# Longer yields for the mixer streams, and MoBA's rotary tied behind the end of RWKV's triangular inverse

## The chip, the cores and the metric

The kernel runs on one core of a Trainium2 chip. The metric is the device time of one execution in microseconds (us); the median of three runs of the kernel before is 927.18 us. PE is the matmul engine (TensorE), DVE the vector engine, ACT the scalar engine, POOL is GpSimd, and SP issues most of the DMAs. Every engine runs its own list of instructions in the order in which the built program holds them, and waits at an instruction until what it reads is there.

## The reference

A trunk of two layers on 256 tokens of width 1024, in float32. In each layer a normed input h is projected once, and the columns go to four token mixers of width 256 and to four gates of width 1024:

```python
y_n = mixer_n(h @ W_in)            # n: stick-breaking attention, RWKV-7, MoBA, HGRN2
mix = sum(sigmoid(gate_n(h)) * (y_n @ W_br[n]) for n in range(4))
x   = x + mix @ W_out
x   = x + swiglu_ffn(rms_norm(x))
```

MoBA attention has four heads of 64. Of each head's query and key the first 16 columns are rotated before the scores:

```python
x1, x2 = t[..., :half], t[..., half:ROPE_DIM]
t = concatenate([x1 * cos - x2 * sin, x2 * cos + x1 * sin, t[..., ROPE_DIM:]])
```

RWKV-7 is a recurrence with a matrix state, S_t = S_{t-1} diag(w_t) + (S_{t-1} a_t) b_t^T + v_t k_t^T and y_t = S_t r_t. The kernel computes it in two chunks of 128 tokens, c = 0 and 1, which needs the inverse of a triangular matrix per chunk and head. HGRN2 is a gated linear recurrence, followed by an RMS norm per head and an output gate.

## The kernel before

**Weights and matmuls.** A float32 weight of 128x1024 is loaded by SP (`load_raw`), rounded to fp32r by a cast on ACT (L128, `hi`), and what the rounding lost is subtracted out on DVE (L129, `lo`). Each product is three matmuls: hi by h-high, lo by h-high, hi by h-low. In the listings a projection therefore shows as `pa<-hi,h` and `pa<-lo,h` at L80 (the one line that issues matmuls; L89 issues transposes). Four raw buffers and four split pairs are in use at a time, and three accumulators `pa`.

**A layer.** `phase` holds the projections, gates and branches as a list of units, and two streams that run beside them: one is RWKV, the other is stick-breaking attention, then MoBA, then HGRN. `merge` and `ffn` follow when units and streams are empty. The mixer stretch is about 50 to 251 us in layer 0 and 503 to 705 us in layer 1.

**What sets the order.** `drive` writes the program. It keeps a model clock pe[0], advanced by an estimate for each matmul. A stream yields a number, its estimate of how long the other engines will need, and is taken up again when pe[0] has passed that number times LATK, 1.7. Until then `drive` issues the next step of a unit. So larger yields put more projection matmuls between two steps of a stream. The clock exists only while the program is being built. On the engines other than PE the instructions then stand in an order that the building framework makes from priorities and dependences; `tc.issue_after(x)` ties what is issued within it behind instruction x.

**RWKV around the change.** `pair_scores` (L530 to 542) makes four matmuls and two predicated copies on DVE (L542); it is called for LB (c = 0, 1), and, after LB has been sent through DRAM to `xb`, for LK (c = 0, 1). The inverse of the small triangular blocks (L571 to 598) is a chain of DVE multiplies (L592) and reduces (L595) over 64 partitions, in three levels. Its result `yb` goes to DRAM (L600) and comes back as `cb` (L603), both issued on ACT's queue, and L607 spreads it over blocks, L617 transposes. The last steps, per chunk, end at L788, with a yield of 200 at L790; `y_T` (L792) transposes the output and splits it into `y` high and low.

**MoBA and HGRN.** MoBA's rotary is L981 to L984 for query and key: a shuffle on DVE, a multiply with sin on DVE, one with cos on POOL, an add on DVE. Then, for the token halves t = 0 and 1, scores (L924 to 930), softmax (L991 to 998), a yield, transposes (`flip_att`), the product with v. HGRN's projection ends in `use_n` (L811 to 814: two reads of the accumulator on ACT, a multiply on DVE, one on POOL); L813 frees its accumulator. Its stream runs seven levels and ends, for t = 0 and 1, in products (L903, L905), a square on ACT (L907), a reduce (L909), an inverse root (L262 on DVE, L263 on POOL), two multiplies (L912, L913), a yield of 3500 (L916) and `y_T` (L917). A branch unit (L1019 to 1034) multiplies a mixer's `y` with its weight, as soon as that `y` is there by the model.

Of the kernel before, what the change touches and what calls it, by code (L numbers as in the profile page):

```python
# [15 lines left out]
OP = mybir.AluOpType  # L16
AX = mybir.AxisListType
# [22 lines left out]
SWAP = [*range(8, 16), *range(8), *range(16, 32)]  # L40
# [6 lines left out]
def trunk(ctx, tc, x, w_t, w_n, w_br, w_out, w_gu, w_dn, par, lora, rows, gains, consts, masks, out):  # L47
    nc = tc.nc
# [14 lines left out]
    def g2d(t, a):  # L63
        return t.rearrange("p (a t) -> p a t", a=a)
# [4 lines left out]
    def over(t, n):  # L69
        return t[:, None, :].to_broadcast([128, n, t.shape[-1]])  # L70
# [124 lines left out]
    for i in range(20):  # L195
        nc.tensor.matmul(warm[:, 0:256], flat1[:, 0:128], flat1[:, 0:256], start=True, stop=True)
        if i in (8, 12):
            c = (i - 8) // 4
# [10 lines left out]
    cosT = cn[:, K_COS:K_COS + 256]  # L209
    sinT = cn[:, K_SIN:K_SIN + 256]  # L210
# [52 lines left out]
        nc.gpsimd.tensor_tensor(dst, dst, half[:, :dst.shape[-1]], op=OP.pow)  # L263
        return e

    last, tail, y1 = [None, None], [], []

    def norm_stats(t):
        y = sb("b2", D)
# [195 lines left out]
    def rwkv(m, l, yT):  # L465
# [100 lines left out]
        for c in range(2):  # L566
            LK.append(g2d(sb("b1", 1024), 4))
            pair_scores(kh, LK[c], c)
            yield 2400
        yield 500  # L570
        nc.vector.tensor_copy(yb.rearrange("p s t -> p (s t)")[:, 1::34],  # L571
                              xb.rearrange("p s t -> p (s t)")[:, 1::34])
        tmp = sb("xy", 512)[0:64]
# [1 line left out]
        for lev in range(1, 4):  # L575
            hb = 1 << lev
            nb = 8 // hb

            def blk(q, i, j):
                return bass.AP(tensor=q.tensor, offset=q.offset + i * hb * 16 + j * hb,  # L580
                               ap=[q.ap[0], [34 * hb, nb], [16, hb], [1, hb]])

            pr = tmp[:, 0:nb * hb ** 3].rearrange("p (b i c k) -> p b i c k", b=nb, i=hb, c=hb)
            t4 = th[:, 0:nb * hb * hb].rearrange("p (b i c) -> p b i c", b=nb, i=hb)
            parts = [(slice(None), i) for i in range(hb)] if hb < nb else [(b, slice(None)) for b in range(nb)]
            bc = [64, nb if hb < nb else hb, hb, hb]

            def product(dst, l4, r4):
                r4 = r4.rearrange("p b k c -> p b c k")
                for b, i in parts:  # L590
                    r = r4 if hb < nb else r4[:, b, None]
                    nc.vector.tensor_tensor(pr[:, b, i], l4[:, b, i, None].to_broadcast(bc), r.to_broadcast(bc),  # L592
                                            op=OP.mult)
                for b, i in parts:
                    nc.vector.tensor_reduce(dst[:, b, i], pr[:, b, i], axis=AX.X, op=OP.add)  # L595

            product(t4, blk(yb, 0, 0), blk(xb, 0, 1))
            product(blk(yb, 0, 1), t4, blk(yb, 1, 1))
# [132 lines left out]
        for c in range(2):  # L731
            p = ps("p1")
            for hp in range(2):
                for a in (2 * hp, 2 * hp + 1):
                    d = slice(a * 64, (a + 1) * 64)
                    mm_cols(p[:, d], LK[c][:, a, 0:128], vn[:, c, d], a == 0, c == 0 and a == 3)
                if c:
                    mm(p[:, hp * 128:(hp + 1) * 128], AR[:, 2 * hp + c, 0], st[:, hp], False, hp == 1)
            rh = sb("h1", 256)
            nc.scalar.copy(rh, p[:, 0:256])  # L740
            yield 1000
            p = ps("p1")
            for a in range(4):
                d = slice(a * 64, (a + 1) * 64)
                mm_cols(p[:, d], Y[c][:, a], rh[:, d])
            u = sb("h1", 256)
            nc.scalar.copy(u, p[:, 0:256])
            yield 1000
            if c == 0:
                p = ps("p1")  # L750
                for a in range(4):
                    o = p[hrow(a), (a // 2) * 64:(a // 2) * 64 + 64]
                    d = slice(a * 64, (a + 1) * 64)
                    mm(o, bkn[:, 0, d], u[:, d], True, False)
                    mm(o, bkn[:, 1, d], vn[:, c, d], False, True)
                st = g2d(sb("h1", 256), 2)
                nc.gpsimd.memset(st, 0.0)
                for hp in range(2):
                    for e in range(2):
                        s = hrow(e)  # L760
                        nc.vector.tensor_scalar(st[s, hp, s], p[s, hp * 64:(hp + 1) * 64], fac[s, hp:hp + 1],
                                                None, op0=OP.mult)
            p = ps("p1")
            for hp in range(2):
                for a in (2 * hp, 2 * hp + 1):
                    d = slice(a * 64, (a + 1) * 64)
                    mm_cols(p[:, d], LK[c][:, a, 128:256], vn[:, c, d], a == 0, False)
                if c:
                    mm(p[:, hp * 128:(hp + 1) * 128], AR[:, 2 * hp + c, 1], st[:, hp], False, False)
                for a in (2 * hp, 2 * hp + 1):  # L770
                    d = slice(a * 64, (a + 1) * 64)
                    mm_cols(p[:, d], LB[c][:, a, 128:256], u[:, d], False, a == 3)
            yv = g2d(p[:, 0:256], 4)
            mean = sm.tile([128, 4], F32, name="mean")
            nc.vector.tensor_reduce(mean, yv, axis=AX.X, op=OP.add)
            nc.vector.tensor_scalar(mean, mean, 1.0 / 64, None, op0=OP.mult)
            yc = sb("h1", 256)
            ycv = g2d(yc, 4)
            nc.vector.tensor_tensor(ycv, yv, bcast(mean, 64), op=OP.subtract)
            y2 = sb("h1", 256)  # L780
            nc.scalar.activation(y2, yc, AF.Square)
            var = sm.tile([128, 4], F32, name="var")
            nc.vector.tensor_reduce(var, g2d(y2, 4), axis=AX.X, op=OP.add)
            rsqrt_small(var, var, 1.0 / 64, 64e-5)
            nc.vector.tensor_tensor(ycv, ycv, bcast(var, 64), op=OP.mult)
            nc.vector.tensor_tensor(yc, yc, gnw, op=OP.mult)
            nc.vector.tensor_tensor(yc, yc, bonus[:, c], op=OP.add)
            nc.vector.tensor_tensor(yc, yc, g[:, c], op=OP.mult)  # L788
            ys.append(yc)
            yield 200  # L790
        yield 6000
        yT[1] = y_T(ys, "p1"), pe[0] + 2500  # L792

# [25 lines left out]
    def hgrn(m, l, yT):  # L819
# [79 lines left out]
        for t in range(2):  # L899
# [13 lines left out]
            nc.vector.tensor_tensor(y, y, gs[:, t], op=OP.mult)  # L913
            ys.append(y)
            yield 300
        yield 3500  # L916
        yT[3] = y_T(ys, "p2"), pe[0] + 2500  # L917

    def scores(q, k, t, mask):
# [56 lines left out]

    def moba(m, v, yT):
        r = []
        for u in m:
            o = g2d(sb("c2", 512), 2)  # L980
            nc.vector.stream_shuffle(o, g2d(u, 2), SWAP)  # L981
            nc.vector.tensor_tensor(o, o, over(sinT, 2), op=OP.mult)
            nc.gpsimd.tensor_tensor(g2d(u, 2), g2d(u, 2), over(cosT, 2), op=OP.mult)
            nc.vector.tensor_tensor(o, o, g2d(u, 2), op=OP.add)  # L984
            r.append(o)
        yield 5000
        po = ps("p3")
        for t in range(2):
# [7 lines left out]
                                     accum_out=den[:, a:a + 1])  # L996
            nc.vector.reciprocal(den, den)
            nc.vector.tensor_tensor(z, z, bcast(den, n), op=OP.mult)
            yield 5000 + 2500 * t
            ts = []  # L1000
            flip_att(z, t, ts)
            yield 1200
# [294 lines left out]
```

## Time and profile before

| | before |
|---|---|
| median of 3 runs | 927.18 us (926.2 to 927.2) |
| the profiled execution | 927.26 us |
| its span, first to last instruction | 925.5 us |
| PE busy | 905.9 us, 98% |
| DVE busy | 647.4 us, 70% |
| ACT busy | 475.2 us, 51% |
| POOL busy | 84.7 us, 9% |
| TensorE's mean granted clock | 0.999 |

The span leaves out some 1.8 us of the execution's own time, before the first and behind the last instruction. PE's row counts an instruction from its start to its modelled end; consecutive matmuls overlap, so that a gap is best read from the starts of neighbours. Idle time of another engine costs nothing unless PE waits for what comes out of it.

### The profile page before, as it was taken

How to read it: one execution, taken by the hardware profiler on the slowest of the kernel's cores; microseconds unless marked ns; L12 is line 12 of the kernel's file. 1: busy time of each engine (PE TensorE's matmuls, PEld its weight loads, DVE VectorE, ACT ScalarE, POOL GpSimd, SP SyncE). 2: the span in 40 equal slices, each digit the busy share in tenths (PEclk: the TensorE clock that was granted, in tenths of full speed). 3: DMA queues.
4: the chain of work that ended last, by engine and by line, in shares of the span. 5: the costliest groups of instructions: out<-in, count | busy, mean ns of one | idle time of the engine just before them, and what ended most of it. 6: DMA issues, size and time to landing. Idle time of an engine off the chain costs nothing.

```text
span 925.5 us, 15008 instructions
## 1 busy us (share of the span) xinstructions
PE 905.9 (98%) x5902; PEld 758.4 (82%) x5902; DVE 647.4 (70%) x957; ACT 475.2 (51%) x726; POOL 84.7 (9%) x94
## 2 busy tenths in 40 slices
PE   8999999999999999999999999999999999999996
PEld 5999677778888888888889986777887888888885
DVE  6668877876766666668567778867778566666665
ACT  6564375355535455556345636644455445545453
POOL 3011100333000000000000201032230000000000
PEclk9999999999999999999999999999999999999999
DMA  8644453345864566667435544433467356656551
GB/s 308 222 147 152 121 169 128 102 155 176 266 205 138 181 190 196 182 204 267 144 115 160 161 138 144 142 123 124 131 211 253 112 184 204 189 184 195 182 182 46
DMA packets 50424, 158.11 MB, mean 171 GB/s; under 512 B 9393, under 2 KB 11953, under 8 KB 50354
## 3 DMA queue, kind: packets, MB, share of 16 engines
q1 hardware_dynamic: 43632, 155.19, 52.7%
q10 hardware_dynamic: 6722, 1.97, 0.9%
q8 instruction: 46, 0.75, 0.3%
q14 instruction: 24, 0.20, 0.1%
HBM read 154.91 MB, written 2.23 MB: 170 GB/s over the span
## 4 chain that ended last, share of the span: by engine, by line
PE 83%; DVE 8%; DMA 4%; issue 2%; ACT 2%; POOL 0%; SPq 0%; ACTq 0%; POOLq 0%; DVEq 0%
PE pa L80 58%; PE p L80 23%; DVE lo L129 2%; DMA raw<-in_w_n_dram 1%; PE p L89 1%; PE pa L89 1%; DMA h<-flat 1%; DMA tri<-yb 1%; DMA flat<-b 1%; DMA raw<-in_w_gu_dram 1%; DVE b L966 1%; ACT hi L128 0%; DVE b L542 0%; DVE c L129 0%; DVE c L981 0%
## 5 line engine op out<-in xcount | busy, mean ns | idle before, releaser
L129 DVE TENSOR_TENSOR lo<-raw,hi 128x1024 fp32r<-128x1024 f32 x268 | 330.2, 1237 | 162.6 <-ACT hi L128 159.7
L128 ACT CAST hi<-raw 128x1024 fp32r<-128x1024 f32 x268 | 279.1, 1048 | 238.5 <-PE pa L80 118.4
L80 PE MATMUL pa<-h,hi 128*128 128x256 f32 (+1 forms) x1280 | 277.9, 339 | 0.0
L80 PEld LDWEIGHTS pa<-h,hi 128*128 128x128 f32 x1280 | 215.9, 190 | 24.6 <-issue 2.0
L80 PE MATMUL pa<-hi,h 128*128 128x512 f32 x576 | 193.4, 400 | 2.2 <-DVE p L813 2.2
L80 PE MATMUL pa<-h,lo 128*128 128x256 f32 x960 | 179.9, 283 | 0.0
L80 PEld LDWEIGHTS pa<-h,lo 128*128 128x128 f32 x960 | 148.6, 191 | 7.0 <-issue 0.7
L80 PEld LDWEIGHTS pa<-hi,h 128*128 128x128 f32 x576 | 108.1, 188 | 27.6 <-DVE p L813 3.0
L80 PE MATMUL p<-hi,c 128*128 128x512 f32 (+1 forms) x352 | 113.4, 394 | 0.0
L80 PE MATMUL pa<-lo,h 128*128 128x512 f32 x288 | 112.7, 391 | 0.0
L80 PEld LDWEIGHTS p<-hi,c 128*128 128x128 f32 x352 | 66.1, 189 | 15.2 <-DVE c L129 0.6
L80 PE MATMUL p<-lo,c 128*128 128x512 f32 (+1 forms) x176 | 69.2, 393 | 0.0
L80 PEld LDWEIGHTS pa<-lo,h 128*128 128x128 f32 x288 | 54.2, 188 | 10.0 <-issue 0.3
L263 POOL TENSOR_TENSOR rs<-rs,half 128x1 f32<-128x1 f32 x10 | 6.0, 595 | 471.6 <-DVE rs L262 471.6
L80 PE MATMUL pa<-hi,y 128*128 128x512 f32 x128 | 43.9, 399 | 0.0
L80 PE MATMUL p<-hi,b 128*128 128x512 f32 x128 | 41.5, 396 | 0.2 <-DVE b L129 0.2
L80 PEld LDWEIGHTS p<-lo,c 128*128 128x128 f32 x176 | 33.1, 188 | 6.8
L1034 POOL TENSOR_TENSOR p<-p,gt 128x512 f32<-128x512 f32 x16 | 31.2, 1973 | 54.3 <-DVE gt L1032 54.3
L340 DVE TENSOR_TENSOR gt<-gt,pa 128x256 f32<-128x256 f32 x80 | 33.1, 414 | 0.0
L128 ACT CAST c<-xy 128x512 fp32r<-128x512 f32 x20 | 12.4, 620 | 39.2 <-DVE xy L1137 39.2
L339 ACT COPY gt<-pa 128x256 f32<-128x256 f32 x80 | 29.3, 366 | 0.0
L80 PEld LDWEIGHTS pa<-hi,y 128*128 128x128 f32 x128 | 24.0, 188 | 6.3 <-issue 1.0
(276 smaller groups left out, 936.5 us busy)
## 6 DMA issues: line engine op xcount, KB each, us to landing
raw<-in_w_gu_dram SPq DMA_DIRECT2D x88, 512.0 KB, 3.7
raw<-in_w_n_dram SPq DMA_DIRECT2D x80, 512.0 KB, 3.5
raw<-in_w_dn_dram SPq DMA_DIRECT2D x44, 512.0 KB, 3.5
raw<-in_w_t_dram SPq DMA_DIRECT2D x40, 512.0 KB, 3.6
raw<-in_w_br_dram SPq DMA_DIRECT2D x16, 512.0 KB, 3.6
raw<-in_w_out_dram SPq DMA_DIRECT2D x16, 512.0 KB, 4.4
b<-in_gains_dram SPq DMA_DIRECT2D x4, 512.0 KB, 5.2
flat<-b ACTq DMA_DIRECT2D x4, 256.0 KB, 3.2
```

The lines of the kernel that those rows point to most:

```text
L80: nc.tensor.matmul(o, l, r, start=start, stop=stop)
L89: nc.tensor.transpose(o, i, ident)
L128: a = nc.scalar.copy(dst[0], src)
L129: return a, (eng or nc.vector).tensor_tensor(dst[1], src, dst[0], op=OP.subtract)
L263: nc.gpsimd.tensor_tensor(dst, dst, half[:, :dst.shape[-1]], op=OP.pow)
L339: nc.scalar.copy(dst, p[:, 256:512])
L340: nc.vector.tensor_tensor(dst, dst, p[:, 0:256], op=OP.add)
L966: nc.vector.tensor_tensor_scan(kb, kb, reset[t][:, ::-1], 1.0, op0=OP.mult, op1=OP.add)
L1034: e.tensor_tensor(mg[f, t], mg[f, t], g, op=OP.add)
```

## The change

The list `inv` carries the last reduce of the inverse from the RWKV stream to the MoBA stream. MoBA waits in steps of 1000 until it is set, ties the rotary of query and key behind it, and clears it. The yields become longer: 3200 instead of 2400 behind each pair of LK scores, with the yield of 500 behind them dropped; 1500 and 200 instead of 200 and 200 at the end of RWKV's two chunks; 6800 and 8300 instead of 5000 and 7500 behind MoBA's softmax; 4300 instead of 3500 ahead of HGRN's `y_T`. No instruction is added to the arithmetic and none is dropped. From L569 on, lines of the new kernel have a number smaller by one, and larger by two from the rotary on.

```diff
-    last, tail, y1 = [None, None], [], []
+    last, tail, y1, inv = [None, None], [], [], []
...
             pair_scores(kh, LK[c], c)
-            yield 2400
-        yield 500
+            yield 3200
...
                 for b, i in parts:
-                    nc.vector.tensor_reduce(dst[:, b, i], pr[:, b, i], axis=AX.X, op=OP.add)
+                    inv[:] = [nc.vector.tensor_reduce(dst[:, b, i], pr[:, b, i], axis=AX.X, op=OP.add)]
...
             ys.append(yc)
-            yield 200
+            yield 1500 - 1300 * c
...
             yield 300
-        yield 3500
+        yield 4300
         yT[3] = y_T(ys, "p2"), pe[0] + 2500
...
         r = []
+        while not inv:
+            yield 1000
         for u in m:
             o = g2d(sb("c2", 512), 2)
-            nc.vector.stream_shuffle(o, g2d(u, 2), SWAP)
-            nc.vector.tensor_tensor(o, o, over(sinT, 2), op=OP.mult)
-            nc.gpsimd.tensor_tensor(g2d(u, 2), g2d(u, 2), over(cosT, 2), op=OP.mult)
-            nc.vector.tensor_tensor(o, o, g2d(u, 2), op=OP.add)
+            with tc.issue_after(inv[0].ins):
+                nc.vector.stream_shuffle(o, g2d(u, 2), SWAP)
+                nc.vector.tensor_tensor(o, o, over(sinT, 2), op=OP.mult)
+                nc.gpsimd.tensor_tensor(g2d(u, 2), g2d(u, 2), over(cosT, 2), op=OP.mult)
+                nc.vector.tensor_tensor(o, o, g2d(u, 2), op=OP.add)
             r.append(o)
+        inv.clear()
...
-            yield 5000 + 2500 * t
+            yield 6800 + 1500 * t
```

DVE in layer 0, through the third level of the inverse, in the kernel before. `c2_1150` and `c2_1155` are MoBA's query and key, `yb_118` is the inverse, `b1_1122` and `b1_1172` are LK of c = 0 and 1, `lo_...` are low halves of weights:

```order
L981 STREAM_SHUFFLE c2_1150<-p_844 128x512
L981 STREAM_SHUFFLE c2_1155<-p_914 128x512
L542 COPY_PREDICATED b1_1122<-mk_116,p1_1123 128x2x256
L542 COPY_PREDICATED b1_1122<-mk_116,p1_1124 128x2x256
L982 TENSOR_TENSOR c2_1150<-c2_1150,cn_70 128x512
L129 TENSOR_TENSOR y_1141<-p3_780,y_1140 128x512
L984 TENSOR_TENSOR c2_1150<-c2_1150,p_844 128x512
L982 TENSOR_TENSOR c2_1155<-c2_1155,cn_70 128x512
L595 TENSOR_REDUCE yb_118<-xy_1226 64x4x4
L984 TENSOR_TENSOR c2_1155<-c2_1155,p_914 128x512
L595 TENSOR_REDUCE yb_118<-xy_1226 64x4x4
```

The same place in the new kernel, from the last reduce of the inverse to the first L812 (L813 of before; L606 is L607 of before):

```order
L594 TENSOR_REDUCE yb_118<-xy_1226 64x8x8
L983 STREAM_SHUFFLE c2_1248<-p_844 128x512
L983 STREAM_SHUFFLE c2_1253<-p_914 128x512
L984 TENSOR_TENSOR c2_1248<-c2_1248,cn_70 128x512
L984 TENSOR_TENSOR c2_1253<-c2_1253,cn_70 128x512
L986 TENSOR_TENSOR c2_1248<-c2_1248,p_844 128x512
L542 COPY_PREDICATED b1_1168<-mk_116,p1_1169 128x2x256
L542 COPY_PREDICATED b1_1168<-mk_116,p1_1170 128x2x256
L986 TENSOR_TENSOR c2_1253<-c2_1253,p_914 128x512
L129 TENSOR_TENSOR lo_1263<-raw_1260,hi_1262 128x1024
L129 TENSOR_TENSOR lo_1281<-raw_1278,hi_1280 128x1024
L606 TENSOR_TENSOR xy_1412<-h1_1372,mk_116 128x512
```

The rotary has left the inverse and stands in one piece behind it, and the first L606 stands ahead of the first L812, which follows two rows later, behind one more `lo`.

PE at the end of layer 0's mixer stretch, in the kernel before: the end of the 33 projection matmuls, and HGRN's `y_T` (`p2_2348`):

```order
L80 MATMUL pa_2232<-hi_2333,h4_134 128x512
L80 MATMUL pa_2232<-lo_2334,h4_134 128x512
L80 MATMUL pa_2232<-hi_2333,h4_134 128x512
L89 MATMUL p2_2348<-cn_70,h2_2263 128x128
L89 MATMUL p2_2348<-cn_70,h2_2292 128x128
L89 MATMUL p2_2348<-cn_70,h2_2263 128x128
L89 MATMUL p2_2348<-cn_70,h2_2292 128x128
L80 MATMUL pa_2232<-hi_2333,h4_134 128x512
```

The same place in the new kernel: the end of HGRN's second product (`p2_2397`), the last projection matmuls, `y_T` (`p2_2451`), and the first matmuls of the branch that reads it (`y_2456`, the high half):

```order
L80 MATMUL p2_2397<-p_1107,c2_2354 64x64 x2
L80 MATMUL pa_2295<-hi_2367,h4_134 128x512
L80 MATMUL pa_2295<-lo_2368,h4_134 128x512
L80 MATMUL pa_2295<-hi_2367,h4_134 128x512 x2
L80 MATMUL pa_2295<-lo_2368,h4_134 128x512
L80 MATMUL pa_2295<-hi_2367,h4_134 128x512
L89 MATMUL p2_2451<-cn_70,h2_2389 128x128
L89 MATMUL p2_2451<-cn_70,h2_2420 128x128
L89 MATMUL p2_2451<-cn_70,h2_2389 128x128
L89 MATMUL p2_2451<-cn_70,h2_2420 128x128
L80 MATMUL pa_2466<-hi_2462,y_2456 128x512
L80 MATMUL pa_2466<-lo_2463,y_2456 128x512
```

Six projection matmuls are left between HGRN's last product and its transposes, and the branch stands directly behind these; before, 51 projection matmuls stood there too. In layer 1 the new kernel has, at the same place, the four transposes of RWKV's output and 18 projection matmuls, then HGRN's transposes and the branch.

## Rows read from the trace of the kernel before

**Rows 1.** The page's first part (busy, share, instructions) and TensorE's granted clock.

```profile
PE 905.9 (98%) x5902; PEld 758.4 (82%) x5902; DVE 647.4 (70%) x957; ACT 475.2 (51%) x726; POOL 84.7 (9%) x94
...
PEclk9999999999999999999999999999999999999999
```

**Rows 2.** PE's waits: who waited for whom, us in total, times, longest.

```profile
PE p L89 <- DVE c L998: 2.7, 2, 1.4
PE pa L80 <- DVE p L813: 2.2, 2, 1.1
...
PE p L80 <- DVE b L542: 1.5, 2, 0.7
PE p L80 <- DVE h L761: 1.0, 1, 1.0
```

**Rows 3.** Timeline of DVE, layer 0: start, us, engine, line, out<-in, idle before.

```profile
99.00 0.99 DVE L982 TENSOR_TENSOR c<-c,cn 128x512 f32<-128x512 f32 x1
...
101.12 0.68 DVE L982 TENSOR_TENSOR c<-c,cn 128x512 f32<-128x512 f32 x1
...
108.90 0.67 DVE L595 TENSOR_REDUCE yb<-xy 64x64 f32<-64x512 f32 x1
...
110.82 0.42 DVE L813 TENSOR_TENSOR p<-p,pa 128x256 f32<-128x256 f32 x1
...
116.42 1.28 DVE L607 TENSOR_TENSOR xy<-h,mk 128x512 f32<-128x512 f32 x2
```

**Rows 4.** Timeline of PE in the same stretch.

```profile
106.55 0.72 PE L80 MATMUL p<-c,c 64*128 64x128 f32 x8
107.20 0.50 PE L80 MATMUL pa<-hi,h 128*128 128x512 f32 x1
...
109.83 0.39 PE L80 MATMUL pa<-hi,h 128*128 128x512 f32 x1
111.30 0.50 PE L80 MATMUL pa<-hi,h 128*128 128x512 f32 x1 [1.08 <-DVE p L813]
```

**Rows 5.** POOL's timeline there; landing times of L600, then of L603.

```profile
97.31 2.14 POOL L983 TENSOR_TENSOR p<-p,cn 128x512 f32<-128x512 f32 x2 [16.46 <-DVE c L981]
...
DMA to landing us min/median/max: 3.4/3.4/3.4
...
DMA to landing us min/median/max: 2.6/2.8/3.0
```

**Rows 6.** Timeline of PE at MoBA's first transposes, layer 0.

```profile
118.01 0.39 PE L80 MATMUL pa<-hi,h 128*128 128x512 f32 x1
119.84 0.63 PE L89 MATMUL p<-cn,c 128*128 128x128 f32 x4 [1.45 <-DVE c L998]
```

**Rows 7.** Timelines of ACT and DVE at HGRN's end, layer 0.

```profile
198.20 0.39 ACT L907 ACTIVATE h<-p 128x256 f32<-128x256 f32 x1 [1.95 <-PE p L80]
200.83 0.42 DVE L913 TENSOR_TENSOR h<-h,p 128x256 f32<-128x256 f32 x1
202.31 0.41 DVE L909 TENSOR_REDUCE hvar<-h 128x4 f32<-128x256 f32 x1
204.51 0.43 DVE L913 TENSOR_TENSOR h<-h,p 128x256 f32<-128x256 f32 x1
208.32 0.59 ACT L128 CAST y<-p 128x512 fp32r<-128x512 f32 x1 [0.46 <-PE p L89]
208.94 0.69 DVE L129 TENSOR_TENSOR y<-p,y 128x512 fp32r<-128x512 f32 x1 [0.79 <-ACT y L128]
```

**Rows 8.** The chain of waits in the same stretch: start, us, what.

```profile
199.06 1.08 PE p L80 x32
200.14 7.71 PE pa L80 x33
```

**Rows 9.** Windows at the end: us, busy of PE PEld DVE ACT POOL, clock, DMA, GB/s.

```profile
919.00:922.00 3.00, 0.00 (x0) 0.00 (x0) 1.39 (x4) 1.02 (x3) 0.55 (x1) 1.00 0.10 37
922.00:923.50 1.50, 0.00 (x0) 0.00 (x0) 0.00 (x0) 0.00 (x0) 0.00 (x0) 0.78 0.93 350
```

## Prediction

> **What bounds the kernel now.** I read the page first: the TensorE matmul row is busy 98% of the span and its granted clock is full in all 40 slices [rows 1]. TensorE (PE) runs its instructions in program order, and no matmul is added or dropped, so the change can move the time only through idle gaps of PE. Next I read the table of PE's waits [rows 2]: the gaps are short and few. The four lines that belong to the mixer streams are L998 (MoBA's softmax ahead of its transposes) with 2.7 us, L813 (HGRN's gate, which frees an accumulator of the projections) with 2.2, L542 (the copy out of RWKV's pair scores) with 1.5, and L761 with 1.0; each stands for one or two waits, one in a layer. Third I read the timelines of DVE, ACT and PE around these waits [rows 3 to 6] and around the end of layer 0's mixer stretch [rows 7, 8], because there the order shows the largest moves. Everything below is a count of PE idle time, gained or lost, against the profiled execution's 927.26 us (span 925.5); the median of the three runs is 927.18, so the two can be taken as one.
>
> **The change part by part.** Arithmetic, tiles and transfers are the same. What moves is the order on every engine, by two causes: the rotary is tied behind the last L595 reduce, and the longer yields push the streams' instructions later among the projections.
>
> *1. The inverse's stretch, 95 to 112 us, and the same again in layer 1.* On DVE the two shuffles, the multiplies (0.99 and 0.68 us) and the adds used to lie inside the inverse [rows 3]; now the inverse runs first and the rotary behind it. Within the stretch that ends at the first L813 this is a permutation, with one addition: the first L607 used to stand behind L813, its row starts at 116.42 with two in 1.28 us [rows 3], and now stands ahead of it. So L813, which ended at 110.82 + 0.42 = 111.24 [rows 3], should end about 0.6 later, less what is gained because fewer DVE instructions lie beside POOL's work: about 111.6. PE meanwhile comes to that point sooner. The L542 wait goes (0.73 as listed [rows 2], 0.88 with the 0.15 by which such figures fall short, see 2) because the second group of pair scores stands six matmuls later, and MoBA's four first score matmuls, 106.55 to 107.20 [rows 4], have left the stretch. PE was ready at 109.83 + 0.23 = 110.06 (0.23 is the spacing of such matmuls: 7.71 us for 33 [rows 8]); it would now be ready near 110.06 - 0.88 - 0.65 = 108.5 and wait for about 3.1 us, against 0.88 + 1.24 = 2.1 for both waits before. That is **+1.0 in each layer, +2.0 together**. Bounds: 0 if the matmul that waits for L813 finds its accumulator free earlier, +1.5 if the weight's low half that stands ahead also comes late.
>
> What is queued behind the moved pieces: L600 writes the inverse to DRAM as soon as the last reduce is out; its landing takes 3.4 us and L603, on the same ACT queue, stands until then; L603's own landing takes 2.8 [rows 5]. In the new order both L603 and two casts stand ahead of L811 and L812. The last reduce ended at 108.90 + 0.67 [rows 3]; with the rotary, the second pair of copies and two low halves moved behind it, some 7.4 us, it ends near 102.2. This gives 102.2 + 3.4 + 2.8 = 108.4 plus issue, and DVE comes to L607 near 109.5, so this costs nothing; the cover is about 1 us, and what is lost beyond it delays L813 and PE one for one. POOL's two multiplies L983 (2.14 us) overlap a DVE multiply of 0.99 us where the same form alone takes 0.68 [rows 3, 5]. So an overlapped operation costs 0.3 more; the new order overlaps one or two as before, and I count nothing.
> The Trainium skill, "SBUF — State Buffer", section "Who interferes with whom", says that a DVE instruction with two SBUF inputs contends with a GpSimd instruction that reads SBUF. By that rule both rotary multiplies, now adjacent, could wait for POOL; the rows price that at 0.3 for each, so the sum would be up to 0.3 a layer higher, inside the bounds above.
>
> *2. MoBA's and RWKV's later waits.* MoBA's score and transpose matmuls move some ten microseconds behind, with 42 matmuls of the next gate unit between. The transposes waited at 119.84 behind a matmul that began at 118.01 [rows 6]: 1.83 less a spacing of 0.23 is 1.60 idle, where the table's figure for it is 1.45. So a listed wait understates the gap by 0.15, and L998's 2.7 in two waits stands for 3.0, L761's 1.0 for 1.15. In the new order the work ahead of both grows by more than these waits: **-4.15**. If L761's is only moved it is -3.0; with some smaller waits gone too it is -4.7.
>
> *3. The end of the stretch in layer 0.* HGRN is the last stream, and its yield of 4300 instead of 3500, behind the later start that MoBA gives it, pushes its tail to the end of the projections. Before, 33 projection matmuls, 7.71 us, lay between HGRN's last product and the transposes of its output [rows 8], and 51 more between these and the branch matmuls. Now six projection matmuls are left, and the branch follows at once. The tail's chain is on other engines: the square starts at 198.20 as the first half's product ends, and its last multiply ends at 200.83 + 0.42 = 201.25, so 3.05 us; the second half's reduce stands behind that on DVE and needs from 202.31 to 204.51 + 0.43 = 204.94, so 2.63 [rows 7]. Together 5.7 us from the end of the first product. PE has in that time three projection matmuls (0.7), the second product (1.1) and six projection matmuls (1.4): 3.2. **PE waits 2.5 us**; 3.0 if a low-half subtraction of 1.2 us stands ahead on DVE. Then the transposes are rounded and split: the cast starts at 208.32 and takes 0.59 [rows 7], and the branch's first matmul needs it, **0.8 us** that were covered before. The low half is done 0.7 us later, behind which the first branch matmuls, which need only the high half, fit. Together +3.3, from 2.8 to 4.1.
>
> *4. The end in layer 1.* The same, but with RWKV's four output transposes and 18 projection matmuls between the second product and HGRN's transposes: 0.7 + 1.1 + 0.45 + 18 x 0.23 = 6.4 us against the chain of 5.7, with the split of RWKV's output (0.7) and a low half (1.2) queued on DVE within it. Wait 0 to 1.3, I take 0.6; then the cast, 0.8. Together +1.4, from 0.3 to 2.1.
>
> *5. Other moves.* Weight loads and casts change places on SP and ACT, POOL's L718 and L840 swap, RWKV's and HGRN's middle steps come later among the projections. PE has waits of 0.2 or less there now, and longer yields put more PE work between a step and its answer, so I count nothing.
>
> Sum: 927.26 + 2.0 - 4.15 + 3.3 + 1.4 = 929.8. With all lower bounds: 927.26 + 0 - 4.7 + 2.8 + 0.3 = 925.7. With all upper bounds: 927.26 + 3.0 - 3.0 + 4.1 + 2.1 = 933.5.
>
> **The rivals.** (a) *Slower, as summed*: the waits at L998 and L761 are traded for a longer one at L813 and an uncovered HGRN tail. For it: PE has nothing else left to run at the end, and the chain's length stands in rows. Against it: the removed waits are as large as one of the two ends.
> (b) *No change that can be told*: the gap at L813 does not grow, the tail in layer 1 is covered but for the cast, that in layer 0 waits as counted: 927.26 - 4.15 + 3.3 + 0.8 = 927.2.
> (c) *Faster*: HGRN's tail runs shorter than in the old trace, since DVE and ACT have no projections' weights left to convert and the second half's reduce need not wait for the first half's multiplies; the chain is then the second half's alone, about 2.9 us after the second product's end, against six matmuls' 1.4: a wait of 1.5 in layer 0, none in layer 1, the casts covered in part (0.8 in all). With no growth at L813: 927.26 - 4.15 + 1.5 + 0.8 = 925.4; with the smaller waits gone as well, 924.9. It decides from the point where layer 0's end costs less than 2.3 us. Against it: the order on DVE puts the second half's reduce behind the first half's last multiply.
> (d) *The clock*: at the end of the program PE had no matmul from 919 to 922 us and its granted clock was still 1.00, but 0.78 over 922 to 923.5 [rows 9]; the gaps inside the program, up to 1.6 us at L998, left it at full [rows 1, 6]. A gap of about 3 us at the end of layer 0 lies between. If the clock fell to 1.2 GHz behind it, the branch matmuls that follow would take twice their time until it rises: for ten to eighteen of them at 0.23 us more each 2 to 4 us, near 933.
> The Trainium skill, "TensorE: Matmul & The Clock Gate", section "Part 1: The HAM clock gate", says that an idle TensorE is throttled to half its clock; the rows so far bear out only that this comes after a longer gap than any in the program.
> (e) *The change does not do what it says*: a rotary left inside the inverse would leave the DVE rows as they were; the order shows that it isn't so.
>
> **How the numbers follow.** (a) 0.57, (b) 0.27, (c) 0.12, (d) 0.04. A measurement of this kernel can tell some 0.2%, 1.85 us, from no change. So faster, under 925.3: 0.12; within 925.3 to 929.0: 0.28; slower: 0.60. The likeliest is (a), 929.8. The range, 925.8 to 932.8, leaves out most of (c) and (d) and the corner where all upper bounds meet.
>
> **What would show it.** Right: a PE wait of about 3 us for L813's successor (L812) in each layer; no wait for L998 or L761; one of 2 to 3 us for HGRN's transposes near 208 us and one for its cast; granted clock 1.0 throughout. Wrong: PE busy without a gap at the end of layer 0; L813 ending before 111.3; waits at RWKV's steps that have none now; a DMA, tri or the inverse's return, as releaser.

## The result, and the profile after

The changed kernel takes 941.15 us (median of four runs, 939.6 to 941.9) against 927.19 of the kernel before (median of four runs, 926.2 to 930.0): **14.0 us slower** by the medians. The ratio on record is 1.0129, 95% interval 1.011 to 1.0149, which is 12.0 us (10.2 to 13.8); so the size of the loss is known to some 2 us. Forecast were 929.8 us, slower, and a range up to 932.8: the direction was right, the size was not. The profiled execution took 940.93 us, 13.7 more than that of before.

The page's first lines and PE's granted clock, the lines that answer to [rows 1]:

```profile
span 939.1 us, 14993 instructions
...
PE 915.6 (97%) x5902; PEld 765.3 (81%) x5902; DVE 649.0 (69%) x957; ACT 475.9 (51%) x726; POOL 85.9 (9%) x94
...
PEclk9999999998999999999999998999999999999999
```

The same 5902 matmuls keep PE busy 9.7 us longer, and in two of the 40 slices of 23.5 us, around 220 and 575 us, the granted clock is below full; a third fall, near 115 us, is spread over two slices and shows only in the windows below. So there are two kinds of loss: PE waits longer, and it runs some matmuls at 1.2 instead of 2.4 GHz.

PE's waits, as in [rows 2] (who waited for whom, us in total, times, longest):

```profile
PE pa L80 <- DVE lo L129: 6.2, 2, 3.1
PE pa L80 <- DVE p L812: 2.5, 2, 1.3
PE p L89 <- DVE h L912: 2.3, 2, 2.1
...
PE pa L80 <- ACT y L128: 1.3, 2, 0.7
```

L998 and L761 are gone from the table, L542 too. In their place stand a wait for a weight's low half that was not there before, 3.1 us in each layer, L812 (L813 of before), and the two waits of HGRN's tail that the forecast had, L912 and the cast L128.

**The first stretch.** Timeline of PE, layer 0, where [rows 4] stood before; start, us, then the instruction and the idle time before it:

```profile
108.97 0.61 PE L80 MATMUL pa<-hi,h 128*128 128x512 f32 x2
112.68 0.50 PE L80 MATMUL pa<-lo,h 128*128 128x512 f32 x1 [3.10 <-DVE lo L129]
...
114.05 0.63 PE L80 MATMUL pa<-hi,h 128*128 128x512 f32 x1
115.89 0.79 PE L80 MATMUL pa<-hi,h 128*128 128x512 f32 x1 [1.21 <-DVE p L812]
...
120.24 0.40 PE L80 MATMUL pa<-lo,h 128*128 128x512 f32 x1
```

Counted from start to start, less one spacing of 0.23, the gaps are 3.26 and 1.61, together 4.87 us, against 0.89 + 1.24 = 2.13 before. In layer 1 they are 3.25 and 1.68. The 0.89 of before, at L542, is read from PE's timeline there:

```profile
97.42 0.39 PE L80 MATMUL pa<-hi,h 128*128 128x512 f32 x1
98.54 1.74 PE L80 MATMUL p<-b,c 64*128 64x256 f32 x8 [0.73 <-DVE b L542]
```

DVE's timeline of the changed kernel says why the low half is late, as in [rows 3]:

```profile
105.85 1.27 DVE L984 TENSOR_TENSOR c<-c,cn 128x512 f32<-128x512 f32 x2
108.11 1.57 DVE L986 TENSOR_TENSOR c<-c,p 128x512 f32<-128x512 f32 x1 [0.99 <-POOL p L985]
109.60 1.32 DVE L542 COPY_PREDICATED b<-mk,p 128x512 f32<-128x512 uint8 x2
110.82 0.67 DVE L986 TENSOR_TENSOR c<-c,p 128x512 f32<-128x512 f32 x1
111.41 2.35 DVE L129 TENSOR_TENSOR lo<-raw,hi 128x1024 fp32r<-128x1024 f32 x2
```

and POOL's, as in [rows 5]:

```profile
105.39 3.74 POOL L985 TENSOR_TENSOR p<-p,cn 128x512 f32<-128x512 f32 x2 [21.94 <-DVE c L983]
```

The rotary is now one block, and its first add L986 must wait for POOL's multiply of the same operand: 0.99 us of idle DVE, in which everything behind it stands, the low half of PE's next weight included. Then the add takes 1.57 us where its twin takes 0.67, beside POOL's second multiply. POOL's pair takes 3.74 us instead of 2.14: its first multiply, beside DVE's second shuffle and two multiplies, takes 2.68 us, its second 1.09, as each did before. The wait for POOL and the slowed add cost DVE's row 0.99 + 0.90 = 1.9 us.

What the clock did there, in windows (us, busy of PE, PEld, DVE, ACT, POOL, granted clock, DMA share, GB/s), as in [rows 9]:

```profile
109.40:112.70 3.30, 0.20 (x2) 0.02 (x1) 3.30 (x6) 1.92 (x5) 0.00 (x0) 1.00 0.01 2
112.70:113.60 0.90, 0.90 (x3) 0.74 (x4) 0.90 (x1) 0.00 (x0) 0.00 (x0) 0.84 0.00 0
113.60:115.80 2.20, 1.08 (x3) 0.33 (x1) 2.20 (x5) 0.00 (x0) 0.00 (x0) 0.50 0.84 274
115.80:120.00 4.20, 4.11 (x10) 3.24 (x11) 3.52 (x7) 1.04 (x1) 2.74 (x3) 0.50 0.63 233
120.00:125.00 5.00, 5.00 (x23) 4.15 (x22) 2.38 (x2) 1.06 (x2) 0.00 (x0) 0.99 0.70 210
```

Through this gap the clock reads 1.00; it falls when the work is back, to 0.50, that is 1.2 GHz, and is full again only after 120 us. In between, ten matmuls take 4.35 us (115.89 to 120.24) instead of 2.3, and three more 1.03 instead of 0.69: 2.4 us. In layer 1 the same: 2.4 us.

**The end of layer 0.** PE's timeline at HGRN's transposes, the place of [rows 7, 8]:

```profile
223.94 0.30 PE L89 MATMUL p<-cn,h 128*128 128x128 f32 x1 [0.18 <-DVE h L912]
226.39 0.90 PE L89 MATMUL p<-cn,h 128*128 128x128 f32 x3 [2.15 <-DVE h L912]
227.97 0.80 PE L80 MATMUL pa<-hi,y 128*128 128x512 f32 x1 [0.67 <-ACT y L128]
228.56 0.63 PE L80 MATMUL pa<-lo,y 128*128 128x512 f32 x1
...
233.05 0.40 PE L80 MATMUL pa<-lo,y 128*128 128x512 f32 x1
```

The gaps are 0.34, 2.34 and 0.98. From 227.97 to 233.05 twelve matmuls take 5.08 us instead of 2.75: half clock again, 2.5 us with the transposes. Here the clock fell before the gap was over, as two windows around its end show (columns as above):

```profile
223.90:226.40 2.50, 0.31 (x2) 0.15 (x2) 1.31 (x5) 1.49 (x2) 1.01 (x1) 0.91 0.35 141
226.40:228.00 1.60, 0.93 (x4) 0.52 (x4) 1.13 (x2) 0.59 (x1) 0.00 (x0) 0.50 0.00 0
```

A mean of 0.91 over 2.5 us is some 0.45 us at 0.50, so the fall is near 225.95 us, 1.7 us after the first transpose ended and 0.44 us before the next began. At the end of layer 1 the transposes wait for nothing that can be told, and the cast's gap is 0.84 us, without a fall of the clock.

**The sum.** Idle time: first stretch 4.87 + 4.93 against 2.13 + 2.13, so +5.5; ends +3.7 and +0.8; gone are L998's 1.6 and 1.4, L761's 1.2 and 0.2 and one of 0.4 at L740, -4.7. That is +5.3. Half clock at three places: 2.4 + 2.4 + 2.5 = 7.3. Together 12.6 of the 13.7 us; the last microsecond is not assigned.

### The profile page after: what moved, and what is told of

It is laid out like the page before. It is cut to its first block, busy times and chain, and to the rows that moved or that the text cites. A ratio compares the mean times of both kernels' runs of the same rounds, so it can differ in the third digit from the quotient of the medians.

```text
span 939.1 us, 14993 instructions
## 1 busy us (share of the span) xinstructions
PE 915.6 (97%) x5902; PEld 765.3 (81%) x5902; DVE 649.0 (69%) x957; ACT 475.9 (51%) x726; POOL 85.9 (9%) x94
## 4 chain that ended last, share of the span: by engine, by line
PE 86%; DVE 7%; DMA 3%; issue 2%; POOL 1%; ACT 1%; SPq 0%; POOLq 0%; DVEq 0%; ACTq 0%
PE pa L80 61%; PE p L80 23%; DVE lo L129 2%; PE pa L89 1%; PE p L89 1%; DMA h<-flat 1%; DVE b L542 1%; DMA flat<-b 1%; DMA raw<-in_w_n_dram 1%; POOL p L985 1%; DVE b L965 0%; DVE xy L591 0%; DMA cn<-in_consts_dram 0%; DVE y L129 0%; DVE xr L411 0%
## 5 line engine op out<-in xcount | busy, mean ns | idle before, releaser
L128 ACT CAST hi<-raw 128x1024 fp32r<-128x1024 f32 x268 | 278.9, 1048 | 257.3 <-PE pa L80 143.3
L80 PE MATMUL pa<-hi,h 128*128 128x512 f32 x576 | 196.3, 406 | 2.5 <-DVE p L812 2.5
L80 PEld LDWEIGHTS pa<-hi,h 128*128 128x128 f32 x576 | 110.3, 191 | 29.9 <-DVE p L812 3.9
L80 PE MATMUL pa<-lo,h 128*128 128x512 f32 x288 | 114.8, 399 | 6.2 <-DVE lo L129 6.2
L128 ACT CAST c<-xy 128x512 fp32r<-128x512 f32 x20 | 12.4, 620 | 39.2 <-DVE xy L1140 39.2
L1037 POOL TENSOR_TENSOR p<-p,gt 128x512 f32<-128x512 f32 x16 | 28.5, 1799 | 24.9 <-DVE gt L1035 23.3
```

The lines of the kernel that those rows point to most:

```text
L80: nc.tensor.matmul(o, l, r, start=start, stop=stop)
L128: a = nc.scalar.copy(dst[0], src)
L1037: e.tensor_tensor(mg[f, t], mg[f, t], g, op=OP.add)
```

## The experiments

Theory A: the tied rotary, as one block, delays PE's low half and accumulator in the first stretch; MoBA's and RWKV's later start pushes HGRN's tail past the last projection in layer 0; behind both, TensorE falls to half clock, and this is more than half of the loss. Rivals were that the longer yields alone cost the time, that the slow matmuls are slowed by something other than the gaps, and that the place of the rotary on DVE, not POOL, makes the low half late. The medians below are given as differences to the kernel before, which ran beside each experiment on the same chip (929.0 to 929.6 us there). The changed kernel was not run again beside them: its own difference is +14.0 by the medians, against 927.2, and +12.0 by the ratio on record, so a difference between an experiment and the whole change holds to some 2 us. The ratios given are the recorded ones, with their 95% intervals; they need not be the quotient of the two medians. Line numbers are those of each kernel.

**1. Yields only.** The change without the tie:

```diff
-        while not inv:
-            yield 1000
         for u in m:
             o = g2d(sb("c2", 512), 2)
-            with tc.issue_after(inv[0].ins):
...
-        inv.clear()
```

> The changed kernel with the rotary untied: MoBA does not wait for the inverse, the rotary's order on DVE is free as before, all longer yields stay. Theory A (the tie costs the first stretch: per layer 2.75 us more idle PE and 2.8 us of matmuls at half clock behind it; the rest is the end of layer 0, where this order has 39 projection matmuls, 8.9 us, ahead of HGRN's transposes): 941.15 - 11.1 - 6.2 - 0.9 gives 923 to 927, granted clock 1.0 in all slices. Rival B (the longer yields cost the time, the tie is only order): 934 or more, with half clock still behind a gap near 110 us.

Measured: -0.3 us, 928.84 against 929.18, ratio 0.9995 (0.9983 to 1.0007). Neither number came true. The waits at L998 and L761 are gone, and the tail is covered in both layers, but the gap at L812 grew to 2.44 us in each layer, new ones of 1.05 and 0.78 us stand at L868 and L679, and behind one of the two equal gaps the clock fell. PE's timelines of this kernel, layer 0 and then layer 1:

```profile
113.93 0.50 PE L80 MATMUL pa<-hi,h 128*128 128x512 f32 x1 [2.28 <-DVE p L812]
...
114.51 1.05 PE L80 MATMUL pa<-hi,h 128*128 128x512 f32 x2
...
566.37 0.50 PE L80 MATMUL pa<-hi,h 128*128 128x512 f32 x1 [2.29 <-DVE p L812]
...
566.94 0.63 PE L80 MATMUL pa<-hi,h 128*128 128x512 f32 x2
```

A pair of matmuls from 114.51 takes 1.05 us to its end, the pair from 566.94 takes 0.63, after gaps that differ by 0.01 us. So the yields give back, at L812 above all, nearly all that they gain at L998: they alone do not cost the time.

**2. Tie only.** The kernel before with `inv`, MoBA's wait and the `issue_after`, and all yields as before.

> The kernel before with only the rotary tied behind the inverse; all yields are the old ones. 33 projection matmuls lie between HGRN's product and its transposes as before. Theory A: the first stretch is as in the changed kernel, 2 x (2.75 + 2.8) = 11.1 more, less what L998's wait loses (up to 3): 935 to 938, half clock near 113 and 574 us but none near 228 us. Rival B: within 2 us of the kernel before.

Measured: +5.8 us, 935.01, 1.0073 (1.0058 to 1.0088): at the lower edge of the 935 to 938 forecast, and less above the kernel before than the forecast had, with gaps of 0.93 and 2.54 us in layer 0 and 1.10 and 2.54 in layer 1 in the first stretch, and gaps at L761 of 1.05 and 2.12 us. The low half is not waited for here, and of the two equal gaps again only one brings half clock (the second line; 0.80 us for one matmul against 0.50). It came once more, near 652 us, behind L761's gap of 2.12 us:

```profile
114.61 0.50 PE L80 MATMUL pa<-hi,h 128*128 128x512 f32 x1 [2.38 <-DVE p L813]
...
567.36 0.80 PE L80 MATMUL pa<-hi,h 128*128 128x512 f32 x1 [2.38 <-DVE p L813]
```

The parts do not add: -0.3 and +5.8 make 5.5, and the whole is 12 to 14. The first stretch's gaps in layer 0 are 2.13 before, 2.44 with the yields, 3.47 with the tie and 4.87 with both. And ahead of HGRN's transposes in layer 0 stand 33 projection matmuls before, 39 with the yields, 33 with the tie, and 6 with both: the projections that cover the tail run out only when the delays are stacked.

**3. MoBA's yields set back.**

```diff
-            yield 6800 + 1500 * t
+            yield 5000 + 2500 * t
```

> The changed kernel with MoBA's yields set back to 5000 and 7500; by the order 39 projection matmuls (8.9 us) then lie ahead of HGRN's transposes in layer 0 instead of 6. Theory A: the 2.5 us gap and the half clock behind it near 228 us go (2.6 us), the first stretch stays: 941.15 - 5.1 = 936 (935 to 937). Rival C (the half clock near 228 us is the late echo of something else than the gap there): the gap goes and the slow matmuls stay, 938.5.

Measured: +7.7 us, 936.84, 1.0086 (1.0064 to 1.0108), within theory A's 935 to 937. The gap at HGRN's transposes and the slow matmuls behind it are gone, and of the cast's two waits the one in layer 0 alone is left, a gap of 0.95 us; from the table of PE's waits:

```profile
PE pa L80 <- ACT y L128: 0.8, 1, 0.8
```

By the traces this takes 2.7 us of idle time and 2.5 us of half clock off the end of layer 0, and 0.8 off the end of layer 1. So MoBA's yields on top of the tie bring the uncovered tail about. Whether HGRN's own longer yield has a part in it was not tried in a run.

**4. Zero-weight matmuls in the gaps of the first stretch.** They add zeros to an accumulator that is open anyway:

```diff
         mm(o, lhs[0], rhs[0], start, False)
+        for _ in range(fill):
+            nc.tensor.matmul(o, zr, rhs[0], start=False, stop=False)
...
-                        k == 0, k == KD - 1)
+                        k == 0, k == KD - 1,
+                        (12, 5)[j] if t == 0 and key[0] == "n" and key[2:] == (2, 0) else 0)
```

> The changed kernel with matmuls of a zero weight added into the first gate unit's accumulator, 12 behind its first matmul and 5 behind its fourth, in both layers: they add zeros, and fill the two gaps of the first stretch (12 x 0.229 = 2.75 of 3.26 us, 5 x 0.229 = 1.15 of 1.61) without taking away what the real matmuls wait for. Theory A, clock: the real matmuls start no later, TensorE's granted clock stays at 1.0 behind the gaps, and the 2.8 us of slow matmuls go in each layer: 941.15 - 5.6 = 935.5 (934.5 to 936.5). Rival D (the slow matmuls there are slowed by something else, such as operands or transfers): no change, 941, or later by the added matmuls.

Measured: +8.1 us, 937.25, 1.0089 (1.0069 to 1.0109): 5.9 us less than the whole change by the medians, some 4 by the ratios. That is theory A's direction and not rival D's, if 0.8 us above the top of the forecast. PE's timeline (L122 are the zero matmuls) and one window around it:

```profile
109.58 2.88 PE L122 MATMUL pa<-hi,zr 128*128 128x512 f32 x12
112.86 0.50 PE L80 MATMUL pa<-lo,h 128*128 128x512 f32 x1 [0.40 <-DVE lo L131]
113.20 0.62 PE L80 MATMUL pa<-hi,h 128*128 128x512 f32 x2
113.66 1.31 PE L122 MATMUL pa<-hi,zr 128*128 128x512 f32 x5
...
116.06 0.50 PE L80 MATMUL pa<-hi,h 128*128 128x512 f32 x1 [0.65 <-DVE p L819]
```

```profile
109.00:121.00 12.00, 10.95 (x48) 8.42 (x47) 11.57 (x15) 4.34 (x8) 3.02 (x4) 1.00 0.41 139
```

The low half is waited for as before (the real matmul starts at 112.86, against 112.68 in the changed kernel), the clock stays at 1.00 in both layers, and the matmuls behind start 0.23 us apart. PE does more and the kernel is faster: the slow matmuls are the echo of the gap, not of operands or transfers.

**5. Shuffles and POOL's multiply left free, only the multiply by sin and the add tied.**

```diff
-            with tc.issue_after(inv[0].ins):
-                nc.vector.stream_shuffle(o, g2d(u, 2), SWAP)
-                nc.vector.tensor_tensor(o, o, over(sinT, 2), op=OP.mult)
-                nc.gpsimd.tensor_tensor(g2d(u, 2), g2d(u, 2), over(cosT, 2), op=OP.mult)
+            nc.vector.stream_shuffle(o, g2d(u, 2), SWAP)
+            nc.gpsimd.tensor_tensor(g2d(u, 2), g2d(u, 2), over(cosT, 2), op=OP.mult)
+            with tc.issue_after(inv[0].ins):
+                nc.vector.tensor_tensor(o, o, over(sinT, 2), op=OP.mult)
                 nc.vector.tensor_tensor(o, o, g2d(u, 2), op=OP.add)
```

> The changed kernel with only the multiply by sin and the add tied behind the inverse; the shuffles and POOL's multiply by cos are free to come early. By the order one shuffle then lies ahead of the inverse's third level and one within it. Theory A1 (the low half that PE waits 3.26 us for is late because the first add stands 0.99 us for POOL's 3.74 us pair of multiplies and then takes 1.57 us beside the second): the pair is done before the add, the low half comes 1.9 us earlier, the gap there shrinks to about 1.4 and both gaps together from 4.87 to about 3.5 us; 2.7 us less in the two layers, and up to 5.6 less where the half clock stays away: 5 to 11 us above the kernel before of the same call, against 13.9 for the whole change. Rival E (POOL is not the cause, the mere place of the rotary ahead of the low half is): gap 3 us or more, within 1 us of the whole change.

Measured: +9.1 us, 1.0109 (1.0081 to 1.0137). The gap for the low half is 1.48 us, as forecast, in place of 3.26: most of it was the wait for POOL, though the shuffles moved as well. The gap at L812 grew, to 2.54 from 1.61. Both together are 4.02, more than the 3.5 forecast, since POOL's second multiply still meets DVE's pair of sin multiplies, which take 2.20 us in place of 1.27. DVE's and then PE's timeline:

```profile
105.54 2.20 DVE L985 TENSOR_TENSOR c<-c,cn 128x512 f32<-128x512 f32 x2
107.67 1.28 DVE L986 TENSOR_TENSOR c<-c,p 128x512 f32<-128x512 f32 x2
```

```profile
111.38 0.50 PE L80 MATMUL pa<-lo,h 128*128 128x512 f32 x1 [1.32 <-DVE lo L129]
...
115.18 0.79 PE L80 MATMUL pa<-hi,h 128*128 128x512 f32 x1 [2.38 <-DVE p L812]
```

In its profiled execution the clock fell in the first stretch of both layers, near 115.0 and 572.4 us, and was full again after 3.4 us each time, where the changed kernel's was after 6.8. It did not fall at HGRN's tail (gaps of 0.35, 2.34 and 0.84), where it had fallen in the changed kernel at nearly the same gaps.

**6. The multiply by cos on DVE instead of POOL.**

```diff
-                nc.gpsimd.tensor_tensor(g2d(u, 2), g2d(u, 2), over(cosT, 2), op=OP.mult)
+                nc.vector.tensor_tensor(g2d(u, 2), g2d(u, 2), over(cosT, 2), op=OP.mult)
```

> The changed kernel with the multiply by cos on DVE instead of POOL. Theory A1: no wait for POOL and no slowed add; against 0.99 + 0.9 us saved stand two multiplies of 0.63 on DVE, of which one lies behind the second pair of copies: the low half about 1.2 us earlier, gap about 2.0 and both gaps together about 3.7 instead of 4.87 us; 2.3 us less in the two layers, more where the half clock stays away: 6 to 12 us above the kernel before. Rival E: the multiplies add 1.3 us to DVE's row and both gaps grow: 14 us or more above.

Measured: +9.1 us, 1.0109 (1.0086 to 1.0133), with gaps of 1.93 and 1.93 us in each layer (forecast 2.0, and 3.7 for both). PE's waits, as above:

```profile
PE pa L80 <- DVE lo L129: 3.5, 2, 1.8
PE pa L80 <- DVE p L812: 3.5, 2, 1.8
```

DVE does more and PE waits 1 us less in each layer. So experiments 5 and 6 take 0.85 and 1.0 us off the 4.87. That is a net figure: 5 leaves a slowed multiply on DVE's row, and 6 puts two more multiplies there.

**7. Zero matmuls at HGRN's tail as well.** To experiment 4 are added 17 of 256 columns ahead of HGRN's second transpose and 3 of 512 ahead of the branch, in layer 0.

> The zero-weight matmuls of the earlier run, and in layer 0 also 17 of 256 columns (2.0 us) between HGRN's first and second transpose and 3 of 512 columns (0.7 us) ahead of the branch's first matmul, into accumulators that the real work overwrites. What the real work waits for stays. Theory A: granted clock 1.0 in all slices, the 2.6 us of slow matmuls near 228 us go as well: what is left over the kernel before is idle time alone, 13.9 - 2.8 x 2 - 2.6 = 5.7 (4.5 to 6.5). Rival D: as the earlier run, 8 above the kernel before.

Measured: +4.9 us, 934.54 against 929.64, 1.0061 (1.0038 to 1.0084). The mean granted clock is 0.999, that of the kernel before:

```profile
core 0: 932.9 us, clock 0.999
```

What is left is the idle time; 5.3 was its sum from the traces, and 5.7 the forecast. Of the whole loss, 9.1 us went with the fillers by the medians and 6 by the ratios; the 7.3 read from the slow matmuls of one execution lie between.

**8 to 12. Looking for a better version.** The yields take PE's wait away at L998, so what stands at L812 seemed worth moving. In experiment 8, ACT copies HGRN's gate out of the accumulator, so that DVE's multiply need not free it:

```diff
+            gc = sb("h2", 256)
+            nc.scalar.copy(gc, p[:, 256:512])
-            nc.vector.tensor_tensor(gs[:, t], gs[:, t], p[:, 256:512], op=OP.mult)
+            nc.vector.tensor_tensor(gs[:, t], gs[:, t], gc, op=OP.mult)
```

> The kernel with the longer yields and the rotary untied (the same time as before in its run, with 2.44 us of waiting at L812 in each layer), and HGRN's gate half of the accumulator copied out by ACT (0.37 us each) so that the accumulator is free without DVE's multiply. Theory F (PE waits there for DVE's queue, not for ACT): both waits of 2.44 us and the half clock that came behind one of them go: 4.9 to 7 us below the kernel before. Rival G (ACT's queue, which holds the issue of the inverse's return between the two copies, frees the accumulator no sooner): within 1.5 us of the kernel before.

Measured: +1.0 us, 1.002 (1.0008 to 1.0033): rival G. PE waits 2.28 us for ACT's copy instead of DVE's multiply, and in layer 0 a new gap of 2.45 us stands at a later low half, near 120 us. ACT's timeline:

```profile
109.55 0.49 ACTq L599 DMA_DIRECT2D tri<-yb  x1
110.08 0.37 ACT L810 COPY p<-pa 128x256 f32<-128x256 f32 x1 [5.00 <-DVE yb L594]
```

ACT stood 5.00 us at the issue L599 for the end of the inverse, with an accumulator full behind it. Hence experiments 11 and 12: the two issues on SP, or on POOL.

> The longer yields, rotary untied, the gate half copied out by ACT as in the earlier run, and the inverse's two transfers (out to DRAM and back) issued on SP instead of ACT. Theory J (in that run ACT stood at these issues for the end of the inverse, so that the copies behind them came no sooner): ACT is free to make the copies as the products end, the waits of 2.28 us go, 0.5 to 2 us of waits for low halves may stay in each layer: 2 to 6 us below the kernel before of the same call. Rival K (SP then holds the weights back, or the low halves wait as long on DVE): within 1.5 us of the kernel before, or above it, with a wait for a weight or a low half of 2 us or more.

> The same with the two transfers issued on POOL's queue. Theory J: as with SP, 2 to 6 us below the kernel before. Rival K: the transfers issued by POOL take longer to land than the 3.4 and 2.8 us of before, and DVE's row stands for them: 0 to 4 us above it.

Measured: +4.4 us on SP (1.0050, 1.0031 to 1.0070) and +9.2 on POOL (1.0104, 1.0085 to 1.0122): rival K, on POOL by more than its 0 to 4. The gap for the accumulator is gone in both, one of 1.0 us for a cast on ACT is in its place, and the wait has moved to the next low half, 3.51 us on SP and 4.88 on POOL in layer 0, since L606 now stands ahead of it on DVE and waits for the inverse to come back; DVE's timeline with SP:

```profile
115.84 1.29 DVE L606 TENSOR_TENSOR xy<-h,mk 128x512 f32<-128x512 f32 x2 [3.10 <-DMA h<-tri]
```

In experiments 9 and 10 the rotary's multiply by sin and its add go to POOL too, with the longer yields and in the kernel before:

```diff
-            nc.vector.tensor_tensor(o, o, over(sinT, 2), op=OP.mult)
+            nc.gpsimd.tensor_tensor(o, o, over(sinT, 2), op=OP.mult)
...
-            nc.vector.tensor_tensor(o, o, g2d(u, 2), op=OP.add)
+            nc.gpsimd.tensor_tensor(o, o, g2d(u, 2), op=OP.add)
```

> The longer yields with the rotary untied, and its multiply by sin and its add on POOL too, so that DVE has only the two shuffles of it: four operations of 0.68 to 0.99 us leave DVE's row, which sets the wait of 2.44 us at L812 in each layer. Theory H (the first stretch is bound by the sum of DVE's row): L812 2 us or more earlier even if POOL's six operations, about 1.1 us each, slow two or three of DVE's by 0.3; both waits shrink to about 0.5, the half clock behind them goes: 3 to 6 us below the kernel before of the same call. Rival I (POOL's share of the operands slows DVE as much as is saved, or MoBA's scores wait for POOL): within 1.5 us of the kernel before, with a wait of PE for POOL or as long for L812.

> The kernel before with the same two operations of the rotary on POOL, nothing else. Theory H: its waits at L542 (0.88) and L813 (1.24) shrink or go, those at L998 and L761 stay: 1.5 to 4 us below the kernel before. Rival I: within 1.5 us of it.

Measured: +9.7 us with the longer yields (1.0099, 1.0081 to 1.0118), outside both expectations: MoBA's scores wait 1.91 us for POOL, and PE's gap at L812 is 3.94 us, because L606 stands ahead of it on DVE and waits 4.05 us for the returning inverse; DVE had been idle since 110.2:

```profile
108.99 1.22 DVE L129 TENSOR_TENSOR lo<-raw,hi 128x1024 fp32r<-128x1024 f32 x1 [0.48 <-ACT hi L128]
114.27 0.69 DVE L606 TENSOR_TENSOR xy<-h,mk 128x512 f32<-128x512 f32 x1 [4.05 <-DMA h<-tri]
```

With the old yields: **-1.8 us**, 927.48 against 929.26, 0.998 (0.9968 to 0.9992), the one version that is below both kernels, just. It is not by the reason given: the gaps at L542 and L813 stay (0.86 and 1.40 us), a new one of 0.61 stands at MoBA's scores; what goes is the wait for L998 in both layers (1.6 and 1.4 us), as PE comes to the transposes later behind those gaps:

```profile
121.31 0.39 PE L80 MATMUL pa<-hi,h 128*128 128x512 f32 x1
121.54 0.60 PE L89 MATMUL p<-cn,c 128*128 128x128 f32 x4
```

## Why the prediction was wrong in size

**What held.** Step 2: L998's and L761's waits are gone, -4.3, against -4.15 forecast; -4.7 with a small one at L740. Step 3: the end of layer 0, +3.3 forecast, +3.7 measured, in its two pieces (2.5 forecast for the transposes, 2.34 + 0.34 measured; 0.8 for the cast, 0.98). Step 4: +1.4 forecast, +0.8 measured; the transposes' wait of 0.6 did not come.

**Step 1 was mis-sized**: +2.0 forecast for both layers, +5.5 measured. It treated DVE's row as a permutation, whose only addition was L607, and counted nothing for POOL. But an order that puts the rotary in one block makes its add follow close on POOL's multiplies: 0.99 us of waiting and 0.90 of slowing stand in the row. Experiments 5 and 6, which take one or both away, bring the two gaps of layer 0 to 4.02 and 3.86 us, not to the 3.1 forecast; the difference was not taken apart further. The prediction gave 0.3 for an overlapped operation, from [rows 3, 5], and neither looked for a wait between the two engines nor for what POOL's own operations become when DVE runs beside them (3.74 us for the pair instead of 2.14). It also named L812 as the one wait, with the low half ahead of it as a mere bound; the low half took 3.26 of the 4.87.
The Trainium skill, "SBUF — State Buffer", section "Who interferes with whom", has a DVE instruction with two SBUF inputs contend with a GpSimd instruction that reads SBUF. The traces agree: L986 took 1.57 us beside L985 and 0.67 after it.

**The clock, rival (d), decided the rest.** It had 4 chances in 100, was put at the end of layer 0 alone and at 2 to 4 us. The size was right for one fall, 2.4 to 2.5 us each, though no row stood behind its "ten to eighteen" matmuls; but it came at three places, with 7.3 us in the profiled execution and 6 to 9 by experiment 7. Its small chance leant on gaps of up to 1.6 us that left the clock full and on one event at the end of the program [rows 9], where the last matmul starts at 917.63 us and the clock reads 1.00 up to 922; at HGRN's tail it fell 1.7 us into a gap. The main error is one of consistency: step 1 itself forecast a wait of about 3 us in each layer, the same size as the one for which (d) was considered, and did not ask what the clock would do there. Without it, the idle time alone would have given 927.3 + 5.3 = 932.6 us, at the upper edge of the range; so step 1 used up the range, and the clock left it.
The Trainium skill, "TensorE: Matmul & The Clock Gate", section "Part 1: The HAM clock gate", says that an idle TensorE is put at half its clock; the windows here agree, with 1.00 through the gap from 109.4 to 112.7 us and 0.50 behind it, and experiments 4 and 7 undo it by filling the gaps.

**Whether a gap brings half clock** its length alone does not tell: gaps of 2.44 and of 2.54 us brought it in one layer and not in the other (experiments 1 and 2); the tail's gap of 2.34 us brought it in the changed kernel and in experiments 4 and 6 and not in 5. The 3.25 and 3.26 us gaps of the changed kernel and of experiment 3, each with a second one behind it, did in all four cases. What decides between equal gaps was not tried and stays open. The price varies from run to run too: the mean granted clock of experiment 5's four executions is 0.987 to 0.995.

## What to carry to other kernels

When an in-order PE is 98% busy, price each forecast gap twice, as idle time and as what the clock may take behind it; here the second was the larger half. Before joining two engines' operations into one block, ask which of them now waits for the other and whether both read the same memory at once: the wait lands on whatever stands behind them in the queue, here the low half of the next weight. And two delays that are each covered can together use up the same cover: 33 and 39 matmuls were left by either, 6 by both.

## What the runs showed of the hardware that was not expected

The granted clock can fall behind a gap as well as in it: in the first stretch it was 1.00 in the 3.3 us without work, 0.84 in the first 0.9 us of work, then 0.50 for some 6 us; at HGRN's tail it fell 0.44 us before the work was back. Matmuls with a zero weight, put where PE would stand idle, made the kernel 4 to 6 us faster in the first stretch of both layers and 6 to 9 us with the tail's as well. POOL's multiply of 128x512 took 1.09 us before, 2.68 beside a shuffle and two multiplies of DVE; DVE's add took 0.67 us alone and 1.57 beside POOL's.
